# One core: the small gate rows and the low-rank decays of a GLA/mLSTM block as products of stacked split parts, the running maximum in two parts, diagonal scores as column sums

## The chip, the core and the metric

The kernel runs on one core of one Trainium2 chip. A core has a matrix engine (TensorE, PE in the profile; its weight loads are the row PEld), a vector engine (VectorE, DVE), an activation engine (ScalarE, ACT), a general one (GpSimd, POOL), and a queue engine that here mainly issues transfers (SyncE, SP). Each has its own in-order queue, and they meet through semaphores. Work lies in an on-chip memory of 128 partitions; TensorE writes into a second one, PSUM, of which a tile here has at most 512 fp32 columns, and DVE and ACT evict from there. The metric is the device time of one execution in microseconds, the median of several.

## The reference

One layer of a hybrid backbone block over 512 latent tokens with a prefix of 256 context tokens, width 2048. One input projection feeds two groups of four heads each: gated linear attention (GLA) with a decay per channel, and mLSTM with scalar gates. Both scan the tokens in both directions. Their gated outputs go through an output projection and then a SwiGLU MLP with a 3x3 convolution. The change concerns the decays, the gates and one set of scores:

```python
    dec = jnp.einsum('btr,zrk->zbtk', glr, gla_w_lr) + gla_b_lr[:, None, None, :]
    gla_loga = (jax.nn.log_sigmoid(dec.astype(f32)) / GLA_NORMALIZER).reshape(N_DIR, b, t, GLA_HEADS, GLA_DK)
...
        rel = jnp.where(tril[:, :, None], bcum[:, :, :, None, :] - bcum[:, :, None, :, :], -jnp.inf)
        scores = jnp.einsum('bhjk,bhik,bhjik->bhji', qc, kc, jnp.exp(rel))
...
        m_q = jnp.maximum(inter_log, jnp.max(d_log, axis=-1))
        s = jnp.einsum('bhjk,bhik->bhji', qc, kc) * jnp.exp(d_log - m_q[..., None])
```

`glr` has 16 values a token, the low-rank input of the decays; z is the direction. The mLSTM gates are 16 further values a token (input and forget gate, two directions, four heads). On the diagonal of the GLA scores the decay is 1, so a diagonal score is the plain product of a token's query and key.

## The kernel before, in words

Everything lies with channels on the partitions and tokens along the row. A plain fp32 product is written with fp32 operands; the big projections instead cut each fp32 operand into a rounded high part (type F32R) and the F32R remainder, and add three products of such parts. A plain fp32 product of 128 columns shows as two records in the profile, a product of parts as one. All of them stand under the helper's line L98, transposes under L103; so the profile is read here by the names of the tiles. `a` are the accumulators of the projections, `hi_h`, `lo_h`, `hTh`, `hTl`, `hch`, `hcl` their split operands (weights, latent tokens, context tokens).

The first 200 us compute the modulation and the normalised tokens. The stretch from 200 to about 830 us is the recurrent part: GLA heads 0 to 3, then mLSTM heads 4 to 7. `weave` mixes the steps of a head (a generator; each `yield` ends a step and names how much projection work may follow) with the projection products of the next head, and the order of TensorE's instructions is pinned to the order in which the program writes them. The other engines' order is set by a list scheduler, with some evictions raised in priority. While a GLA head runs, `gla_prep` of the next one is advanced by `next(after, None)` at six places of the levels.

The steps that the change touches:

- `small_rows` turns the gathered rows `gm` into `glr`: latent tokens in columns 0 to 511, context tokens behind them. Rows 0 to 15 are the decays' low-rank input, row 16 is ones (for the bias), rows 32 to 47 are the mLSTM gate inputs.
- `gla_prep` loads the head's weights `wlr` (16 rows and the bias row), forms the decays of the latent tokens `dec` (128 channels by 512 tokens, one product a direction) and of the context tokens `cdec` (tokens by channels, two products a direction, one PSUM tile a direction), and puts both through `log_sigmoid`: three passes of ACT (tiles `lt`, `ct`) and one of DVE (`la`, `cla`). `bt` are the running sums of `la`, `csum` the sums of `cla` by products with triangles of ones, `b` and `ends` follow from `bt`.
- `gla` first forms the diagonal scores: `sd` is query times key of a 128-token block, multiplied by twice the identity into `scd`, the first half of the tile `sc`. Then for seven levels `ex` takes the exponentials of differences of `bt`, times query and key, `sl` is their product, and a mask copies part of it into `sc`. At the end `po` multiplies `qi` and `sc` with states and values.
- `ml_gates` picks from `glr` the four rows of a gate and a direction (`pre`, two products a tile in two groups of columns), runs sums and running maxima along the tokens, writes the negated running maximum `negg` (rows 0 to 3 and 32 to 35 for the two directions), transposes rows into columns (`pa`), and spreads the maximum at the end of the context over the partitions (`pgc`, from `dg`).
- `mlstm` spreads the head's row of `negg` over 128 partitions (`pg`, one product a direction) and takes exponentials from it.

Transfers of projection weights (`raw_h`, 512 KB each) and of `wlr` go through SP's queue in its order. Memory of a pool is handed on when the last reader of the tile before is through.

## Time and profile before

| | |
|---|---|
| median of 3 runs | 2513.63 us (2512.5 to 2513.84) |
| the profiled execution | 2511.87 us, its span 2510.1 us |
| granted clock | 0.998 |
| PE busy | 2469.3 us, 98% |
| DVE, ACT, POOL busy | 1815.0, 1024.0, 182.5 us |
| the recurrent part, 200 to 830 us | 630 us, of which PE busy 622.30 us |

The page has numbered parts: the engines' busy time, the span in 40 slices, the queues, the chain of work that ended last, the costliest groups, and the transfers. A row of a timeline gives start, length, engine, line, operation, written tile and read tiles, partitions x elements and type, and how many instructions of a kind follow each other; in brackets stands how long the engine was idle before, and who ended that. Since products overlap, the step between two starts is what a product costs in a stream, not its length. A row of the chain gives start, length and what it was. Buffer numbers are left out.

### The profile page before, as it was taken

The page shows a single profiled execution, that of the slowest core. Times are in us where ns is not written, and L with a number is a line of the kernel's source. Part 1 is how long each engine was busy: PE and PEld are TensorE (multiplying, and loading weights), DVE is VectorE, ACT ScalarE, POOL GpSimd, SP SyncE. Part 2 cuts the span into 40 slices and gives each one's busy share as a digit, 9 for nine tenths or more (in the row PEclk, how much of TensorE's full clock was granted, in tenths as well). Part 3 has the DMA queues.
Part 4 walks back from the last instruction along what each step waited for, and adds up shares of the span by engine and source line. Part 5 has one row for each costly group of instructions (what it writes and reads, how often), then busy time and mean ns, then how long its engine had stood idle before and what let it go on. Part 6 is the DMA issues. An engine that isn't in the chain of part 4 may idle for free.

```text
span 2510.1 us, 39398 instructions
## 1 busy us (share of the span) xinstructions
PE 2469.3 (98%) x15740; PEld 2204.1 (88%) x15740; DVE 1815.0 (72%) x2880; ACT 1024.0 (41%) x1517; POOL 182.5 (7%) x242
## 2 busy tenths in 40 slices
PE   6999999999999999999999999999999999999998
PEld 4887889888987888888989999999999999999997
DVE  6666754554445877858988787878787878787886
ACT  4224543332213233226454444444444444444445
POOL 0000000000000000000020101010101010101022
PEclk9999999999999999999999999999999999999999
DMA  9741011123334878842373737373636363646464
GB/s 385 271 172 42 26 43 51 51 76 125 110 117 155 286 274 304 299 158 99 108 176 101 168 104 166 107 168 104 167 104 166 107 162 108 161 113 160 113 186 135
DMA packets 121552, 372.20 MB, mean 148 GB/s; under 512 B 13908, under 2 KB 18328, under 8 KB 121368
## 3 DMA queue, kind: packets, MB, share of 16 engines
q1 hardware_dynamic: 94680, 318.29, 37.7%
q0 software_dynamic: 25600, 50.34, 11.4%
q8 instruction: 123, 2.02, 0.3%
q10 hardware_dynamic: 1088, 1.05, 0.1%
q14 instruction: 61, 0.50, 0.1%
HBM read 319.30 MB, written 50.33 MB: 147 GB/s over the span
## 4 chain that ended last, share of the span: by engine, by line
PE 85%; issue 9%; DVE 2%; DMA 2%; POOL 1%; ACT 1%; SPq 0%; DVEq 0%; POOLq 0%; ACTq 0%
PE a L98 19%; PE dn L98 17%; PE uv L98 15%; PE ug L98 14%; PE ga L98 7%; PE po L98 4%; PE wo L98 3%; PE sl L98 1%; PE ps_m L98 1%; DMA raw_m<-in_w_mod 1%; PE cst L98 1%; PE s L98 1%; DMA xl<-in_xT 0%; POOL x2d L1269 0%; DMA x2d<-st 0%
## 5 line engine op out<-in xcount | busy, mean ns | idle before, releaser
L98 PE MATMUL dn<-gh,lo_d 128*128 128x512 f32 x672 | 262.3, 390 | 0.3 <-DVE lo_d L93 0.3
L98 PE MATMUL dn<-gh,hi_d 128*128 128x512 f32 x672 | 261.6, 389 | 0.0
L98 PE MATMUL dn<-gl,hi_d 128*128 128x512 f32 x672 | 261.6, 389 | 0.0
L1215 DVE SCALAR_TENSOR_TENSOR cv<-pads,cwt,cv 128x512 f32<-128x512 f32 x344 | 239.5, 748 | 0.6
L1269 POOL DMA_DIRECT2D x2d<-st x160 | 140.1, 928 | 1142.7 <-ACT st L1268 1057.5
L313 DVE SCALAR_TENSOR_TENSOR sum_m<-raw_m,csil,sum_m 128x512 f32<-128x512 f32 x240 | 180.1, 750 | 9.0 <-DMA raw_m<-in_w_mod 3.1
L93 DVE TENSOR_TENSOR lo_buv<-sum_uv,hi_buv 128x1024 fp32r<-128x1024 f32 x80 | 98.0, 1224 | 103.6 <-ACT hi_buv L92 103.6
L98 PEld LDWEIGHTS dn<-gh,lo_d 128*128 128x128 f32 x672 | 126.1, 188 | 28.9 <-DVE lo_d L93 2.6
L98 PE MATMUL a<-hi_h,hTh 128*128 128x256 f32 x512 | 150.4, 294 | 0.5 <-ACT e L406 0.5
L98 PEld LDWEIGHTS dn<-gl,hi_d 128*128 128x128 f32 x672 | 126.2, 188 | 25.9
L98 PEld LDWEIGHTS dn<-gh,hi_d 128*128 128x128 f32 x672 | 126.2, 188 | 25.6
L98 PE MATMUL a<-hi_h,hTl 128*128 128x256 f32 x512 | 144.7, 283 | 0.0
L98 PE MATMUL a<-lo_h,hTh 128*128 128x256 f32 x512 | 144.7, 283 | 0.0
L92 ACT CAST hi_d<-raw_d 128x1024 fp32r<-128x1024 f32 x86 | 88.6, 1030 | 131.9 <-PE ug L98 70.6
L93 DVE TENSOR_TENSOR lo_d<-raw_d,hi_d 128x1024 fp32r<-128x1024 f32 x86 | 102.9, 1196 | 48.1 <-ACT hi_d L92 47.5
L98 PE MATMUL ug<-bth,hi_bug 128*128 128x256 f32 x480 | 136.7, 285 | 0.1
L98 PE MATMUL uv<-bth,lo_buv 128*128 128x256 f32 x480 | 135.9, 283 | 0.8 <-DVE lo_buv L93 0.8
L98 PE MATMUL uv<-bqh,lo_auv 128*128 128x256 f32 x480 | 135.9, 283 | 0.0
L98 PE MATMUL uv<-bth,hi_buv 128*128 128x256 f32 x480 | 135.9, 283 | 0.0
L98 PE MATMUL uv<-bql,hi_auv 128*128 128x256 f32 x480 | 135.8, 283 | 0.0
L98 PE MATMUL ug<-bqh,lo_aug 128*128 128x256 f32 x480 | 135.8, 283 | 0.0
L98 PE MATMUL uv<-btl,hi_buv 128*128 128x256 f32 x480 | 135.8, 283 | 0.0
(379 smaller groups left out, 7347.2 us busy)
## 6 DMA issues: line engine op xcount, KB each, us to landing
raw_m<-in_w_mod SPq DMA_DIRECT2D x192, 512.0 KB, 5.2
raw_d<-in_w_down SPq DMA_DIRECT2D x82, 512.0 KB, 3.4
raw_ug<-in_w_up SPq DMA_DIRECT2D x80, 512.0 KB, 3.5
x2d<-st POOLq DMA_DIRECT2D x160, 256.0 KB, 5.5
raw_uv<-in_w_up SPq DMA_DIRECT2D x80, 512.0 KB, 6.2
raw_h<-in_w_heads SPq DMA_DIRECT2D x64, 512.0 KB, 3.6
raw_ga<-in_w_gates SPq DMA_DIRECT2D x32, 512.0 KB, 4.5
raw_wo<-in_w_out SPq DMA_DIRECT2D x32, 512.0 KB, 4.8
```

The costliest lines, as they stand in the source:

```text
L92: cast[0] = S.copy(hi, x).ins
L93: return V.tensor_tensor(out=lo, in0=x, in1=hi.bitcast(F32), op=ALU.subtract).ins
L98: ins = PE.matmul(*args, **kw)
L313: V.scalar_tensor_tensor(out=parts[0], in0=x, scalar=ck, in1=parts[0], op0=ALU.mult, op1=ALU.add)
L1215: V.scalar_tensor_tensor(out=t3, in0=src, scalar=w, in1=t3, op0=ALU.mult, op1=ALU.add)
L1269: nc.gpsimd.dma_start(x2d[k], t, accum_op=ALU.add)
```

## The change

Every fp32 number can be written as a sum of an F32R high part and an F32R remainder. The change stacks such parts along the contraction, which is short here, so that one product does what several would:

- `glr` becomes a tile of 98 rows of type F32R: high part of the 32 rows, the high part once more, the remainders, and two rows of ones. One product of `gm` with a selection of 96 columns fills PSUM; ACT casts it into all 96 rows, and DVE makes the last 32 the remainder (a column `C_LO` holds −1 there).
- The weights come as 98 rows in HBM; ACT casts, DVE turns rows 32 to 63 and the last into remainders. The raw tile and `wlr` have one buffer each. High by high, high by remainder and remainder by high are then added by one `dec` or `cdec` product.
- The two directions of `cdec` go into one PSUM tile, two products of 256 columns, and one `log_sigmoid`. The step that fell away is an empty `yield`.
- `pre` selects its 36 rows by a matrix `pick`, which is loaded and cast once, and adds high part and remainder by one product.
- `negg` becomes two F32R tiles, `negh` and `negl`, and `pg` two products a direction.
- `sd`: DVE multiplies query and key into `scd`, and four products with one column of ones sum over the channels; the result is spread along the row by the identity, as before.
- `small`, one tile, holds what `csil` and `eps` held; the constants are 128 columns wider.

```diff
@@ -43,8 +43,9 @@
 
 C_ID, C_LS, C_US, C_SEG = (P * i for i in range(4))
 C_SA = C_SEG + T
-C_ONE = C_SA + 32
-C_END = C_ONE + 1
+C_ONE = C_SA + 96
+C_LO = C_ONE + 1
+C_END = C_LO + 64
 
 
 def constants():
@@ -54,8 +55,20 @@
-    c[:, C_SA : C_SA + 32] = i[:, None] % 32 == np.arange(32)[None, :]
+    c[:, C_SA : C_SA + 96] = i[:, None] % 32 == np.arange(96)[None, :] % 32
     c[:, C_ONE] = 1.0
+    c[64:96, C_LO] = -1.0
+    c[32:64, C_LO + 1] = c[97, C_LO + 1] = -1.0
+    return c
+
+
+def picks():
+    c = np.zeros((96, P), np.float32)
+    for t in range(2):
+        for d in range(2):
+            for r in range(4):
+                c[[16 + 8 * d + 4 * t + r, 80 + 8 * d + 4 * t + r], 36 * t + 32 * d + r] = 1.0
+    c[0:36, 72:108] = np.eye(36)
     return c
 
 
@@ -114,9 +127,9 @@
     cst = keep.tile([P, C_END], F32, name="cst")
     cols = keep.tile([P, 148], F32, name="cols")
     msk = keep.tile([P, len(LEVELS), P], U8, name="msk")
-    csil = keep.tile([P, 128], F32, name="csil")[:, 0:KT]
+    small = keep.tile([P, 128], F32, name="small")
+    csil, eps = small[:, 0:KT], small[:, KT : KT + 1]
-    eps = keep.tile([P, 128], F32, name="eps")[:, 0:1]
@@ -477,12 +490,13 @@
     st_h = ExitStack()
     states = pool(st_h, "states")
 
-    glr = states.tile([48, T + TC], F32, name="glr")
+    glr = states.tile([98, T + TC], F32R, name="glr")
 ...
-    negg = states.tile([36, T], F32, name="negg")
+    pick = states.tile([96, 128], F32R, name="pick")
+    negg = [states.tile([36, T], F32R, name=f"neg{p}") for p in "hl"]
@@ -573,7 +587,10 @@
-    V.memset(glr, 1.0)
+    V.tensor_copy(glr[96:98, :], cst[96:98, C_ONE : C_ONE + 1].to_broadcast([2, T + TC]))
+    pickf = mraw.tile([96, 128], F32, name="pickf", tag="raw")
+    nc.sync.dma_start(pickf, a["picks"])
+    V.tensor_copy(pick, pickf)
@@ -591,11 +608,11 @@
 
     def small_rows():
         for c0, n, m in ((0, T, gm[0]), (T, TC, gm[1])):
-            ps = psb(f"glr{c0}", (48, n))
-            mm(ps[0:16, :], cc(C_SA, 16), m, start=True, stop=True)
-            mm(ps[32:48, :], cc(C_SA + 16, 16), m, start=True, stop=True)
-            V.tensor_copy(glr[0:16, c0 : c0 + n], ps[0:16, :])
-            S.copy(glr[32:48, c0 : c0 + n], ps[32:48, :])
+            ps = psb(f"glr{c0}", (96, n))
+            mm(ps, cc(C_SA, 96), m, start=True, stop=True)
+            o = glr[0:96, c0 : c0 + n]
+            S.copy(o, ps)
+            V.scalar_tensor_tensor(out=o, in0=o.bitcast(F32), scalar=cc(C_LO, 1, 96), in1=ps, op0=ALU.mult, op1=ALU.add)
             yield 1.4
 
 
@@ -652,23 +669,27 @@
 
     def gla_prep(h, out):
 
-        wlr = wk2.tile([17, 2, DK], F32, name=f"wlr{h}", tag="wlr")
-        nc.sync.dma_start(wlr, a["w_lr"][h])
+        raw = wtile(f"wlraw{h}", "wlraw", 2, DK)[0:98]
+        nc.sync.dma_start(raw, a["w_lr"][h])
+        wlr = wk.tile([98, 2, DK], F32R, name=f"wlr{h}", tag="wlr")
+        S.copy(wlr, raw)
+        V.scalar_tensor_tensor(out=wlr, in0=wlr.bitcast(F32), scalar=cc(C_LO + 1, 1, 98), in1=raw,
+                               op0=ALU.mult, op1=ALU.add)
         la = wtile(f"la{h}", "la", 2, T)
         t = wtile(f"lt{h}", "tmp", 2, T)
-        cla = wtile(f"cla{h}", "cla", 2, CJ, DK)
-        ct = ytile(15, f"ct{h}", (P, 2, CJ, DK))
+        cla = wtile(f"cla{h}", "cla", CJ, 2, DK)
+        ct = ytile(15, f"ct{h}", (P, CJ, 2, DK))
         for d in range(2):
             ps = psb(f"dec{h}{d}")
-            mm(ps, wlr[:, d, :], glr[0:17, 0:T], start=True, stop=True)
+            mm(ps, wlr[:, d, :], glr[:, 0:T], start=True, stop=True)
             log_sigmoid(la[:, d], ps, t[:, d])
             yield
-        for d in range(2):
-            ps = psb(f"cdec{h}{d}", (P, CJ, DK))
-            for j in range(CJ):
-                mm(ps[:, j, :], glr[0:17, T + P * j : T + P * j + P], wlr[:, d, :], start=True, stop=True)
-            log_sigmoid(cla[:, d], ps, ct[:, d])
-            yield
+        ps = psb(f"cdec{h}", (P, CJ, 2, DK))
+        for j in range(CJ):
+            mm(ps[:, j], glr[:, T + P * j : T + P * j + P], wlr, start=True, stop=True)
+        log_sigmoid(cla, ps, ct)
+        yield
+        yield
 
@@ -682,9 +703,9 @@
             tri = cc(C_LS) if d == 0 else cc(C_US)
             for j in range(CJ):
                 more = j == d
-                mm(ps[:, d, j, :], tri, cla[:, d, j, :], start=True, stop=not more)
+                mm(ps[:, d, j, :], tri, cla[:, j, d, :], start=True, stop=not more)
                 if more:
-                    mm(ps[:, d, j, :], ones, cla[:, d, 1 - j, :], start=False, stop=True)
+                    mm(ps[:, d, j, :], ones, cla[:, 1 - j, d, :], start=False, stop=True)
@@ -740,11 +761,12 @@
         scd, sc1 = sc[:, 0], sc[:, 1]
-        ps = psb(f"sd{h}", (P, TJ, P))
+        mul(scd.rearrange("p a b -> p (a b)"), *qk)
+        ps = psb(f"sd{h}", (P, TJ))
         for j in range(TJ):
-            mm(ps[:, j, :], qk[1][:, P * j : P * j + P], qk[0][:, P * j : P * j + P], start=True, stop=True)
-        V.scalar_tensor_tensor(out=scd, in0=ps, scalar=2.0, in1=ident.unsqueeze(1).to_broadcast([P, TJ, P]),
-                               op0=ALU.mult, op1=ALU.mult)
+            mm(ps[:, j : j + 1], scd[:, j, :], cst[:, C_ONE : C_ONE + 1], start=True, stop=True)
+        V.scalar_tensor_tensor(out=scd, in0=ident.unsqueeze(1).to_broadcast([P, TJ, P]), scalar=2.0,
+                               in1=ps.unsqueeze(2).to_broadcast([P, TJ, P]), op0=ALU.mult, op1=ALU.mult)
@@ -834,9 +856,7 @@
         for t, r in ((0, li), (1, pf)):
             for c0, n, at in ((0, T, lat0), (T, TC, ctx0)):
                 ps = psb(f"pre{t}{c0}", (36, n))
-                for d in range(2):
-                    e = C_ID + 32 + 8 * d + 4 * t
-                    mm(ps[rows[d], :], cst[32:48, e : e + H], glr[32:48, c0 : c0 + n], start=True, stop=True)
+                mm(ps, pick[:, 36 * t : 36 * t + 36], glr[0:96, c0 : c0 + n], start=True, stop=True)
                 for d in range(2):
                     V.tensor_scalar(out=r[rows[d], at[d] : at[d] + n], in0=ps[rows[d], :],
                                     scalar1=bg[rows[d], t : t + 1], scalar2=None, op0=ALU.add)
@@ -869,8 +889,10 @@
             end = TC - 1 if d == 0 else T
-            V.tensor_scalar(out=negg[rows[d], :], in0=gmx[rows[d], lat0[d] : lat0[d] + T], scalar1=-1.0,
-                            scalar2=None, op0=ALU.mult)
+            x = gmx[rows[d], lat0[d] : lat0[d] + T]
+            nh, nl = (n[rows[d], :] for n in negg)
+            V.tensor_scalar(out=nh, in0=x, scalar1=-1.0, scalar2=None, op0=ALU.mult)
+            V.scalar_tensor_tensor(out=nl, in0=x, scalar=-1.0, in1=nh.bitcast(F32), op0=ALU.mult, op1=ALU.subtract)
             V.tensor_scalar(out=dg[rows[d], :], in0=e, scalar1=gmx[rows[d], end : end + 1], scalar2=None, op0=ALU.mult)
             pg = psb(f"pgc{d}", (P, H))
             mm(pg, cst[rows[d], C_ONE : C_ONE + 1].to_broadcast([H, P]), dg[rows[d], :], start=True, stop=True)
@@ -897,8 +919,9 @@
         for d in range(2):
             rows = slice(32 * d, 32 * d + H)
             pg = psb(f"pg{h}{d}")
-            mm(pg, cst[rows, C_ID + 32 * d + hh : C_ID + 32 * d + hh + 1].to_broadcast([H, P]), negg[rows, :],
-                      start=True, stop=True)
+            one = pick[rows, 72 + 32 * d + hh : 73 + 32 * d + hh].to_broadcast([H, P])
+            for n, part in enumerate(negg):
+                mm(pg, one, part[rows, :], start=(n == 0), stop=(n == 1))
             S.activation(qs[:, d, :], pg, AF.Exp, bias=gccol[:, d, hh : hh + 1])
...
-    lr = np.concatenate([gla_w_lr[0], gla_b_lr[0][:, None, :]], 1)
-    r["w_lr"] = lr.reshape(2, 17, H, DK).transpose(2, 1, 0, 3)
+    lr = np.zeros((2, 98, H * DK), np.float32)
+    for row in range(0, 96, 32):
+        lr[:, row : row + 16] = gla_w_lr[0]
+    lr[:, 96:] = gla_b_lr[0][:, None, :]
+    r["w_lr"] = lr.reshape(2, 98, H, DK).transpose(2, 1, 0, 3)
```

The order on TensorE at head 1's preparation, around the second group of `cdec`, before (`sl_6` are the scores of the seventh level, `a_1` and `a_2` projections):

```order
L98 MATMUL a_1_2035<-hTl_950,hi_h_3_2393 128x512
L98 MATMUL a_1_2035<-hTh_949,lo_h_3_2394 128x512
L98 MATMUL cdec_2409<-wlr_2294,glr 128x128 x2
L98 MATMUL sl_6_2422<-ex_6_2416 128x128 x4
L98 MATMUL a_2_2036<-hi_h_3_2393,hTh_939 128x256
L98 MATMUL a_2_2036<-lo_h_3_2394,hTh_939 128x256
```

and after:

```order
L111 MATMUL a_1_2039<-hTl_951,hi_h_3_2395 128x512
L111 MATMUL a_1_2039<-hTh_950,lo_h_3_2396 128x512
L111 MATMUL sl_6_2417<-ex_6_2411 128x128 x4
L111 MATMUL a_2_2040<-hi_h_3_2395,hTh_940 128x256
L111 MATMUL a_2_2040<-lo_h_3_2396,hTh_940 128x256
```

The group has gone, its products having been joined to the first group; `sl_6` follows `a_1` directly.

The order on SP, where the loads of `wlr` for heads 0 and 1 stand, before:

```order
L179 DMA raw_h_0_2045<-in_w_heads 128x1024
L656 DMA wlr_2080<-in_w_lr 17x256
L179 DMA raw_h_1_2149<-in_w_heads 128x1024
L656 DMA wlr_2294<-in_w_lr 17x256
L179 DMA raw_h_2_2264<-in_w_heads 128x1024
L179 DMA raw_h_3_2391<-in_w_heads 128x1024
L179 DMA raw_h_4_2507<-in_w_heads 128x1024
L179 DMA raw_h_5_2678<-in_w_heads 128x1024
L656 DMA wlr_2745<-in_w_lr 17x256
L179 DMA raw_h_6_2801<-in_w_heads 128x1024
```

and after:

```order
L192 DMA raw_h_0_2048<-in_w_heads 128x1024
L192 DMA raw_h_1_2147<-in_w_heads 128x1024
L192 DMA raw_h_2_2263<-in_w_heads 128x1024
L192 DMA raw_h_3_2393<-in_w_heads 128x1024
L192 DMA raw_h_4_2502<-in_w_heads 128x1024
L192 DMA raw_h_5_2674<-in_w_heads 128x1024
L673 DMA wlraw_2082<-in_w_lr 98x256
L673 DMA wlraw_2293<-in_w_lr 98x256
L192 DMA raw_h_6_2800<-in_w_heads 128x1024
L673 DMA wlraw_2741<-in_w_lr 98x256
```

The loads of heads 0 and 1 have moved from behind the first and second `raw_h` of the piece to behind the sixth, where `raw_h_6` follows them; the load of head 2 now stands behind `raw_h_6` instead of ahead of it.

The order on DVE around head 1's diagonal scores, before (`ob` takes the output of head 0 from `po`, `sc` from `sd` is the diagonal, `qi` belongs to head 1):

```order
L818 COPY ob_2536<-po_0_2537 128x256
L818 COPY ob_2536<-po_1_2546 128x256
L818 COPY ob_2536<-po_2_2561 128x256
L84 TENSOR_TENSOR qi_2704<-qi_2704,e_0_1256 128x1024
L818 COPY ob_2536<-po_3_2570 128x256
L746 SCALAR_TENSOR_TENSOR sc_2589<-sd_2593,cst 128x512
```

and after:

```order
L840 COPY ob_2531<-po_0_2532 128x256
L840 COPY ob_2531<-po_1_2541 128x256
L840 COPY ob_2531<-po_2_2556 128x256
L97 TENSOR_TENSOR sc_2584<-e_0_1257,e_1_1266 128x512
L97 TENSOR_TENSOR qi_2700<-qi_2700,e_0_1257 128x1024
L840 COPY ob_2531<-po_3_2565 128x256
L768 SCALAR_TENSOR_TENSOR sc_2584<-cst,sd_2589 128x512
```

The product of query and key into `sc` stands behind the third `ob` and ahead of `qi`; the evictions from `po` and `sd` follow in the order that they had.

More of the change, by code (lines that the diff above doesn't have):

```diff
@@ L1393, in arrange @@
     r["masks"] = masks()
+    r["picks"] = picks()
     r["cols"] = np.concatenate([col(g_norm1[0]), col(g_norm2[0]), col(b_mod[0]), col(g_final), col(gla_g_norm[0]),
```

## The prediction

> **What bounds the kernel now.** I read the page's head and busy lines first, then a table of windows over the stretch in which the edited lines run, then the waits of TensorE there.
>
> ```profile
> span 2510.1 us, 39398 instructions
> PE 2469.3 (98%) x15740; PEld 2204.1 (88%) x15740; DVE 1815.0 (72%) x2880; ACT 1024.0 (41%) x1517; POOL 182.5 (7%) x242
> ```
>
> ```profile
> 200.00:222.00 22.00, 18.57 (x105) 13.75 (x100) 13.42 (x28) 11.94 (x23) 0.00 (x0) 1.00 0.08 26
> 222.00:262.00 40.00, 39.08 (x247) 34.33 (x247) 35.79 (x57) 22.75 (x46) 0.00 (x0) 1.00 0.08 28
> 262.00:330.00 68.00, 66.78 (x395) 59.20 (x394) 46.17 (x89) 34.01 (x77) 0.00 (x0) 1.00 0.10 32
> 330.00:405.00 75.00, 75.00 (x461) 67.62 (x460) 40.46 (x63) 31.91 (x62) 0.73 (x1) 1.00 0.14 43
> 520.00:830.00 310.00, 309.52 (x1704) 267.63 (x1704) 156.47 (x332) 87.88 (x168) 15.38 (x33) 1.00 0.38 124
> ```
>
> ```profile
> PE sl L98 <- DVE ex L84: 3.2, 3, 1.7
> PE cdec L98 <- DVE la L635: 1.7, 2, 1.1
> ```
>
> The columns of the windows are length, then PE, PEld, DVE, ACT and POOL busy, granted clock (1.00 in all), DMA share and GB/s. PE has no free time from 330 to 405 and half a microsecond from 520 to 830, so a microsecond taken off PE there is one off the end. From 200 to 222 it is idle for 3.4 us, and in 222:262 DVE is busy for 35.8 of 40: there the vector chain decides, and the waits name it (columns: total, times, longest). The sum is made against the profiled execution, 2511.87 us (1.76 us around the span), and is carried to the median of 2513.63 us by the same 1.76 us.
>
> **Unit prices.** From the timeline of PE (start, length; the step between starts is the price, since lengths overlap):
>
> ```profile
> 481.18 0.28 PE L98 MATMUL a<-hi_h,hTl 128*128 128x256 f32 x1
> 481.30 0.28 PE L98 MATMUL a<-hi_h,hTh 128*128 128x256 f32 x1
> ...
> 487.86 0.39 PE L98 MATMUL a<-hTl,hi_h 128*128 128x512 f32 x1
> 488.08 0.39 PE L98 MATMUL a<-hTh,lo_h 128*128 128x512 f32 x1
> 488.40 1.02 PE L98 MATMUL pre<-glr,cst 16*4 16x512 f32 x4
> 489.35 0.50 PE L98 MATMUL a<-hTh,hi_h 128*128 128x512 f32 x1
> ...
> 490.94 0.60 PE L98 MATMUL pre<-glr,cst 16*4 16x256 f32 x4
> 491.47 0.39 PE L98 MATMUL a<-hi_h,hTh 128*128 128x256 f32 x1
> ```
>
> The `a` products are split parts, as the new `dec`, `cdec`, `pre` and `pg` are: one record costs 0.12 us at 256 columns and 0.22 to 0.23 us at 512. The chain has the plain ones:
>
> ```profile
> 234.18 1.05 PE dec L98 x2
> ...
> 298.12 0.65 PE cdec L98 x4
> ```
>
> **dec and cdec.** A `dec` falls from 1.05 to 0.23 us: −0.82 each, two a head. A head's `cdec` falls from two groups of 0.65 to two records of 0.12: −1.06. That is −2.7 us of PE a head, four heads. What of it arrives:
>
> - 330:405 prepares head 3, with PE never idle: −2.7, whole.
> - 262:330 prepares head 2; its last third waits for vector work after `cdec`. The two `dec` count whole (−1.6), of `cdec` I take two thirds (−0.7): −2.3, bounds −1.0 and −2.7.
> - Head 0 and the preparation of head 1, 200:262. The chain of head 0 and its tail:
>
> ```profile
> 206.15 1.06 PE dec L98 x2
> ...
> 209.53 0.70 DVE la L635
> ...
> 221.82 1.13 PE sl L98 x8
> ```
>
> ```profile
> 251.58 0.43 DVE cla L635
> 252.05 1.60 PE csum L98 x12
> ```
>
> From 206.15 on the chain leaves PE and goes through ACT and DVE until 221.82, so head 0's 2.7 us mostly become wait. Only the start of the first decay moves up, since both `dec` no longer stand before the ACT work; I take −0.4. Then head 1's preparation frees 2.7 us of PE, but DVE (89% busy) gains one `cla` of 0.43 us that becomes part of a longer one, loses 0.43 us to the new weight part (same size, so the same row), and still has to bring `ex` to the next `sl`. What comes free is that `csum` no longer waits for the second `cla` at 252.05. I take −1.6, so −2.0 for the window, with bounds 0 (the vector chain keeps its time) and −3.9 (2.7 of PE, the 0.9 us that PE idles in 222:262, and 0.3 more at head 0).
>
> **pre.** The rows give 0.95 and 0.53 us, two each: 2.96. After: 0.23 + 0.12, twice, 0.70. Each group has an empty 0.09 us ahead of it (488.08 + 0.23 to 488.40), and about as much behind: up to 0.7 more. So −2.3 to −3.0; I take −2.7. Behind it stands a chain that does not get shorter:
>
> ```profile
> 505.48 0.41 DVE L872 TENSOR_SCALAR negg<-pf 4x512 f32<-4x512 f32 x1
> 506.69 0.21 DVE L874 TENSOR_SCALAR dg<-cst,pf 4x4 f32<-4x4 f32 x1
> ```
>
> ```profile
> 507.11 0.53 PE L103 MATMUL pa<-cst,li 4*128 4x4 f32 x6
> 507.75 0.36 PE L98 MATMUL pgc<-dg,cst 4*128 4x4 f32 x2
> ```
>
> `pgc` needs `dg`, done at 506.90: 0.85 us of slack. PE comes 2.7 earlier. DVE comes between 0 and 2.7 earlier (it evicts the same four tiles); I take 2.0. The low half of the maximum adds one DVE operation of 0.41 ahead of `dg`. Slack 0.85 − 0.41 − 0.7 = −0.3: a new wait of 0.3 us. So −2.4, bounds −1.5 and −3.0.
>
> **pg.** Timeline of PE at the first of the four heads:
>
> ```profile
> 519.72 0.28 PE L98 MATMUL a<-hi_h,hTl 128*128 128x256 f32 x1
> 519.93 1.13 PE L98 MATMUL pg<-negg,cst 4*128 4x512 f32 x4
> 520.99 0.44 PE L98 MATMUL a<-hi_h,hch 128*128 128x384 f32 x1
> ```
>
> Both directions, four records, take 1.06 us, as long as the single `dec` with two: they run side by side, in two groups of rows. Four split records take 0.92 us in file and 0.47 in two pairs side by side. The nearest row is `pg` itself, on the same rows, so I take side by side, with a little for gaps: −0.55 a head, −2.2 for four; bounds −0.6 and −2.4. The second negation itself is the 0.41 us counted above.
>
> **sd.** Four products of 128 columns become one DVE product (`q` times `k`) and four products of one column:
>
> ```profile
> 271.05 1.89 PE L98 MATMUL po<-v,sc 128*128 128x256 f32 x8
> 272.78 1.05 PE L98 MATMUL sd<-e,e 128*128 128x128 f32 x8
> 273.59 0.36 PE L98 MATMUL a<-hi_h,hTh 128*128 128x256 f32 x1
> ```
>
> ```profile
> 1140.64 3.10 PE L98 MATMUL ps_rms<-cst,sqsq 128*128 128x1 f32 x24 [0.21 <-DVE sqsq L87]
> ```
>
> A record of `sd` costs 0.81 / 8 = 0.10 us; one with a single column costs 3.10 / 24 = 0.13 us in the row of `ps_rms`. So eight of them save nothing; bounds 0 and +0.2 a head. The Trainium skill, TensorEngine Tiling (Array Packing), section Performance Considerations, says that a product of one column takes as long as one of 60, about 60 cycles; at the 2.4 GHz of its page TensorE: Matmul & The Clock Gate eight records would by that take some 0.2 us (an estimate), and the sum would fall by 2.4 us more. The row of `ps_rms` disagrees.
>
> The new DVE product writes into the tile that the previous head's `po` reads. In heads 0, 2 and 3 it stands many operations ahead of `sd`. In head 1 `sd` follows `po` directly. The reads of that tile end about a quarter into the group at 271.05, some 271.6; an evict of the same 128x512 size (`la`, 0.70) brings 272.3 plus hand-overs. `sd` wants PE at 272.78: no wait, bound +1.0 if the release comes with the group's end. Four extra products of 0.7 lie in DVE's idle time.
>
> **glr, weights, constants.** `glr` goes from two products side by side to one wider one, and the evictions are two passes over 96 rows instead of one copy each; PE has `a` behind it: 0. The constants load grows by 65.5 KB, at the start, when PE waits for loads. The weights' load grows to 100 KB and moves down SP's queue, behind the fourth `raw_h`:
>
> ```profile
> raw_h<-in_w_heads SPq DMA_DIRECT2D x64, 512.0 KB, 3.6
> ```
>
> ```profile
> 170.91 24.02 SPq L179 DMA_DIRECT2D raw_h<-in_w_heads  x4
> ...
> 218.25 28.26 SPq L179 DMA_DIRECT2D raw_h<-in_w_heads  x3
> ```
>
> By the landing row 65.5 KB cost at most 0.5 us; I take +0.2. The fourth `raw_h` is issued at 194.9, so head 0's weights land by about 199 to 203, then a cast and a DVE pass (0.4 each), and `dec` wants them at 206.15: hidden with 2 us or more. Later heads ask for theirs tens of microseconds ahead.
>
> **Sum.** −2.0 − 2.3 − 2.7 − 2.4 − 2.2 + 0 + 0.2 = −11.4 us: the profiled execution at 2500.5, the median at 2502.2 us.
>
> **Rivals.**
> - *All of it arrives.* Eight `dec` 6.6, four `cdec` 4.2, `pre` 3.0, `pg` 2.4, and about 1 us of the waits on DVE: −17.2 + 0.2, 2496.6 us. For it: PE at 98%. Against: the chain through ACT and DVE from 206 to 222.
> - *The vector chains keep their time, and `pg` runs in file.* 200:262 nothing, 262:330 −1.0, 330:405 −2.7, `pre` −1.5, `pg` −0.6, `sd` +1.0 at head 1, preparation +0.5, start +0.5: −3.8, 2509.8 us. For it: DVE at 89% in 222:262.
> - *One column is next to free*: `sd` gives back its whole 0.81 us in four heads, −3.2 on top of the sum: 2499.0 us. Against: 0.13 us a record in `ps_rms`. It is the rule of the Trainium skill's tiling page, above, taken to its end.
> - *Slower: head 0's weights come late.* SP's queue stands before the `raw_h` of 218.25 for a buffer. If the weights' load is held until then (it also waits for memory that PE must have left), it lands at 218.6 + 3.6, is ready 0.8 later at 223.0, and `dec` starts 16.9 us late, all of it PE standing: −11.4 + 16.9, 2519.1 us. It decides from 16.4 us of lateness on (`dec` at 222.6). Against: in SP's order it stands ahead of that `raw_h`, not behind.
>
> **How the numbers follow.** Changes under 0.2% (5.0 us) can't be told from none. Chances: the forecast 0.50 (own range 2499 to 2505.5), all of it 0.17, one column cheap 0.04, vector chains 0.19, late weights 0.10. The first three are faster (0.71), and a quarter of the vector case, whose terms spread over 2506 to 2512, is too (0.05): 0.76 faster, 0.14 within, 0.10 slower. The range takes in the first case whole, nearly all of "all of it" and most of the vector case, and leaves out late weights and the tails: 2495.5 to 2511.
>
> **What would show it.** In the profile after: `dec` at 0.23 us a record, `cdec` at 0.12, and the head 3 stage shorter by 2.7; `pre` 0.2 and 0.1; four `pg` records within 0.5 us (in file: 0.9); `sd` still near 0.8; head 0's `sl` only some 0.4 earlier, with a wait on ACT or DVE ahead of it; a short wait at `pgc`. Wrong would be: a wait of PE at head 0's `dec` for the weights, one at head 1's `sd` for the DVE product, or `sd` at a quarter of its time.

## The result and the profile after

The changed kernel takes 2503.59 us (median of five runs, 2501.22 to 2507.01) against 2513.63 us: ratio 0.9964, 95% interval 0.9953 to 0.9975. That is 10.0 us less, where 11.4 were forecast (2502.2 us, range 2495.5 to 2511). In a second comparison both were slower, with the same ratio: 2506.02 against 2514.87 us, 0.9964 (0.9953 to 0.9976).

The profiled execution is one of the slow ones of its kernel: 2507.01 us, span 2505.3. The span is therefore only 4.8 us shorter than before, so the two profiles are compared stage by stage. First the page's head and the windows that answer to those of before (length, then PE, PEld, DVE, ACT and POOL busy, granted clock, DMA share, GB/s):

```profile
span 2505.3 us, 39311 instructions
PE 2458.9 (98%) x15692; PEld 2205.6 (88%) x15692; DVE 1819.1 (73%) x2887; ACT 1021.3 (41%) x1509; POOL 182.2 (7%) x242
```

```profile
200.00:222.00 22.00, 17.67 (x102) 14.48 (x95) 14.02 (x28) 11.93 (x22) 0.00 (x0) 0.92 0.11 34
222.00:262.00 40.00, 37.54 (x246) 34.65 (x246) 37.46 (x60) 22.79 (x44) 0.00 (x0) 1.00 0.10 32
330.00:405.00 75.00, 75.00 (x477) 69.91 (x476) 40.34 (x67) 29.76 (x59) 0.74 (x1) 1.00 0.16 50
```

The clock in the first row is 0.92, where it was 1.00. In 222:262 DVE has come to 37.5 us of 40 and PE's free time has grown from 0.9 to 2.5 us: the chain there is a vector chain now. From 330 to 405 PE still has no free time.

Since TensorE's order is the same, the same instruction can be looked up in two timelines. Starts on PE, in us; the last two columns are the shift against before in the changed kernel (its first profile, and its second, of the run `after_again` below):

| first start of | before | after | shift | shift, second profile |
|---|---|---|---|---|
| `glr` | 199.94 | 200.54 | +0.60 | +0.92 |
| `dec`, head 0 | 206.08 | 206.11 | +0.03 | +0.34 |
| `po`, head 0 | 261.03 | 259.54 | −1.49 | −1.65 |
| `yt`, head 1 | 330.73 | 327.62 | −3.11 | −3.29 |
| `yt`, head 2 | 410.97 | 404.40 | −6.57 | −6.75 |
| `pre` | 484.08 | 477.50 | −6.58 | −6.76 |
| `pa` | 507.11 | 497.60 | −9.51 | −9.69 |
| `pg`, head 4 | 519.93 | 514.79 | −5.14 | −5.48 |
| last `yt` | 814.39 | 807.59 | −6.80 | −7.13 |
| `ug` (after the second norm) | 1148.74 | 1143.28 | −5.46 | −5.86 |

The gain grows as forecast up to `pa`, then 4.4 us of it are lost between `pa` and `pg` (4.2 in the second profile), and another 1.3 us at the second norm. The products themselves are as cheap as forecast. From the timeline of PE (start, length, idle before in brackets):

```profile
359.25 0.40 PE L111 MATMUL a<-hTh,lo_h 128*128 128x512 f32 x1
359.49 0.39 PE L111 MATMUL dec<-glr,wlr 98*128 98x512 f32 x1
359.72 1.05 PE L111 MATMUL sl<-ex 128*128 128x128 f32 x8
...
364.74 0.28 PE L111 MATMUL a<-hi_h,hTl 128*128 128x256 f32 x1
364.86 0.40 PE L111 MATMUL cdec<-wlr,glr 98*128 98x256 f32 x2
365.10 1.06 PE L111 MATMUL sl<-ex 128*128 128x128 f32 x8
...
480.31 0.40 PE L111 MATMUL pre<-glr,pick 96*36 96x512 f32 x1
480.54 0.40 PE L111 MATMUL a<-hTh,hi_h 128*128 128x512 f32 x1
...
481.94 0.28 PE L111 MATMUL pre<-glr,pick 96*36 96x256 f32 x1
482.06 0.29 PE L111 MATMUL a<-hi_h,hTh 128*128 128x256 f32 x1
```

`dec` costs 0.23 us, both records of `cdec` 0.24, `pre` 0.23 and 0.12. The gaps ahead of these products (0.09 us before) are gone too. Behind `pa` the profile shows what went wrong:

```profile
497.60 0.53 PE L116 MATMUL pa<-cst,li 4*128 4x4 f32 x6
498.55 0.41 PE L116 MATMUL pa<-cst,cum 4*128 4x4 f32 x4 [0.42 <-DVE cum L100]
499.38 0.35 PE L111 MATMUL pgc<-dg,cst 4*128 4x4 f32 x2 [0.43 <-DVE dg L896]
...
500.83 0.28 PE L111 MATMUL a<-hi_h,hTh 128*128 128x256 f32 x1
500.95 0.35 PE L111 MATMUL a<-lo_h,hTh 128*128 128x256 f32 x1
501.09 0.42 PE L111 MATMUL a<-hi_h,hTl 128*128 128x256 f32 x1
501.92 0.80 PE L116 MATMUL pa<-cst,li 4*128 4x4 f32 x6 [0.41 <-DVE gccol L899]
...
504.31 0.41 PE L111 MATMUL a<-hi_h,hTh 128*128 128x256 f32 x1
504.52 0.41 PE L111 MATMUL a<-lo_h,hTh 128*128 128x256 f32 x1
```

There are three waits of 0.4 us, and from 501 on an `a` record of 256 columns costs 0.21 us instead of 0.12. Only the first two waits lie ahead of 501; the third falls into the slower stretch. The windows of the same profile give the granted clock of that stretch:

```profile
496.00:501.00 5.00, 4.15 (x31) 3.42 (x30) 4.91 (x9) 1.46 (x4) 0.00 (x0) 1.00 0.00 0
501.00:508.00 7.00, 6.59 (x33) 6.28 (x33) 2.07 (x8) 1.07 (x4) 0.00 (x0) 0.51 0.26 77
508.00:512.00 4.00, 4.00 (x22) 3.49 (x21) 2.42 (x6) 1.50 (x3) 0.00 (x0) 1.00 0.00 0
```

For 6.8 us the granted clock is half. That is the larger part of the 4.4 us: 1.3 of waits, some 3.1 of clock. While TensorE has work, the clock fell below 0.97 in three places of this profile: 211 to 214 us (head 0, behind a wait of 1.8 us for `la` ahead of `cdec`), 501 to 508, and 1136 to 1143 us (behind `ps_rms`). Before, it fell in one, at 1143 to 1147 us. DVE's timeline shows what PE waits for:

```profile
497.21 0.41 DVE L894 TENSOR_SCALAR negh<-pf 4x512 fp32r<-4x512 f32 x1
497.56 0.94 DVE L100 TENSOR_TENSOR cum<-cum,pf 36x768 f32<-36x768 f32 x1
498.42 0.67 DVE L895 SCALAR_TENSOR_TENSOR negl<-pf,negh 4x512 fp32r<-4x512 f32 x1
499.02 0.21 DVE L896 TENSOR_SCALAR dg<-cst,pf 4x4 f32<-4x4 f32 x1
```

The new `negl` stands ahead of `dg`, for which `pgc` waits, but behind `cum`, for which the first wait is. DVE's first negation starts 8.27 us earlier than before (505.48), PE's `pa` 9.51: DVE has come up less than PE.

### The profile page after: what moved, and what is told of

The parts are those of the page before. It is cut to its first block, busy times and chain, and to the rows that moved or that the text cites. A ratio compares the mean times of both kernels' runs of the same rounds, so it can differ in the third digit from the quotient of the medians.

```text
span 2505.3 us, 39311 instructions
## 1 busy us (share of the span) xinstructions
PE 2458.9 (98%) x15692; PEld 2205.6 (88%) x15692; DVE 1819.1 (73%) x2887; ACT 1021.3 (41%) x1509; POOL 182.2 (7%) x242
## 3 DMA queue, kind: packets, MB, share of 16 engines
q0 software_dynamic: 25600, 50.34, 11.4%
q10 hardware_dynamic: 1088, 1.05, 0.1%
## 4 chain that ended last, share of the span: by engine, by line
PE 84%; issue 9%; DVE 3%; DMA 2%; ACT 1%; POOL 0%; SPq 0%; DVEq 0%; POOLq 0%; ACTq 0%
PE a L111 18%; PE uv L111 16%; PE dn L111 15%; PE ug L111 15%; PE ga L111 7%; PE po L111 4%; PE wo L111 3%; PE sl L111 1%; PE ps_m L111 1%; DVE cv L1238 1%; DMA raw_m<-in_w_mod 1%; DMA raw_uv<-in_w_up 1%; PE cst L111 1%; PE s L111 1%; DVE lo_d L106 0%
## 5 line engine op out<-in xcount | busy, mean ns | idle before, releaser
L326 DVE SCALAR_TENSOR_TENSOR sum_m<-raw_m,small,sum_m 128x512 f32<-128x512 f32 x240 | 180.1, 750 | 10.3 <-DMA raw_m<-in_w_mod 4.8
```

The costliest lines, as they stand in the source:

```text
L326: V.scalar_tensor_tensor(out=parts[0], in0=x, scalar=ck, in1=parts[0], op0=ALU.mult, op1=ALU.add)
```

## The experiments

Two theories stood after the first profile. The clock theory: PE's new waits at `pa` and `pgc`, which come from DVE, pull the clock down, and taking them away brings 4 us. The chance theory: half clocks come at random places and only the 1.3 us of waits belong to the change.

**The changed kernel again.**

> The changed kernel once more, to see whether its stretches of half granted clock come at the same places. If PE's new waits cause them (theory 1), the granted clock is again 0.50 for 3 to 7 us right behind the waits at the start of head 0 (about 210 us) and at pa and pgc (about 501 us), and pg starts near 514.8. If they come by chance (theory 2), they lie elsewhere or are absent, and pg starts near 511.5.

Measured: 2506.02 us (2501.94 to 2507.97, six runs). Its profile has the half clock at the same place (from 500.4 to 507.3 us), none at head 0, and the one at the second norm; `pg` starts at 514.45. Ahead of the half clock stand the first two waits, at `cum` and `dg`; the third is absent:

```profile
496.00:501.00 5.00, 4.15 (x29) 3.47 (x28) 4.91 (x9) 1.46 (x4) 0.00 (x0) 0.94 0.00 0
501.00:508.00 7.00, 6.92 (x36) 6.61 (x35) 1.90 (x8) 1.21 (x5) 0.00 (x0) 0.55 0.24 77
```

So the place behind `pa` repeats, the one at head 0 doesn't, though its wait of 1.8 us ahead of `cdec` is the same. Two profiles of kernels below that keep the two waits (`u_sd`, `u_cdec`) have 6.8 us of half clock there as well.

**The parts of the maximum formed late (`m1`).**

```diff
-            V.tensor_scalar(out=nh, in0=x, scalar1=-1.0, scalar2=None, op0=ALU.mult)
-            V.scalar_tensor_tensor(out=nl, in0=x, scalar=-1.0, in1=nh.bitcast(F32), op0=ALU.mult, op1=ALU.subtract)
...
-            V.tensor_copy(gccol[:, d, :], pg)
+            spread = V.tensor_copy(gccol[:, d, :], pg).ins
             yield 1.4
+        for d in range(2):
+            x = gmx[rows[d], lat0[d] : lat0[d] + T]
+            nh, nl = (n[rows[d], :] for n in negg)
+            with tc.issue_after(spread):
+                V.tensor_scalar(out=nh, in0=x, scalar1=-1.0, scalar2=None, op0=ALU.mult)
+                V.scalar_tensor_tensor(out=nl, in0=x, scalar=-1.0, in1=nh.bitcast(F32), op0=ALU.mult,
+                                       op1=ALU.subtract)
```

> The changed kernel with both parts of the negated running maximum formed behind the last gccol, so that dg and cum come earlier on DVE and PE's order stays. Theory 1: PE's waits at pa and pgc fall from 1.3 us to about 0.3, the half clock at 501 us goes, pg starts 4 us earlier, near 510.8; the time falls by up to 4 us against the changed kernel, to about 2500 us. Theory 2: only the waits go, pg near 513.8, the half clock still comes in some executions.

Measured: 2502.59 us (2501.09 to 2503.69), 3.4 us under the changed kernel of the same batch. PE's waits are down to 0.2 us, and the clock stays whole. Timeline of PE, and windows, of `m1`:

```profile
497.15 0.53 PE L116 MATMUL pa<-cst,li 4*128 4x4 f32 x6
497.90 0.41 PE L116 MATMUL pa<-cst,cum 4*128 4x4 f32 x4 [0.21 <-DVE cum L100]
498.17 0.36 PE L111 MATMUL pgc<-dg,cst 4*128 4x4 f32 x2
500.08 0.53 PE L116 MATMUL pa<-cst,li 4*128 4x4 f32 x6
```

```profile
496.00:501.00 5.00, 4.79 (x42) 4.06 (x40) 4.35 (x9) 1.45 (x6) 0.00 (x0) 1.00 0.11 23
501.00:508.00 7.00, 7.00 (x43) 6.48 (x43) 5.26 (x14) 2.35 (x7) 0.00 (x0) 1.00 0.17 61
```

From `pa` to `pg` the shift goes from −9.96 to −9.57 us: 0.4 lost where the changed kernel loses 4.4. This is what the clock theory expects, to 0.4 us (`pg` at 510.36, expected 510.8). One profile could be chance, but all thirteen of this document agree: the four with waits of 0.4 us at both `cum` and `dg` have the half clock behind them, and of the eight others without a wait made by hand (five with one wait of 0.2 us, `u_pg` with one of 0.4, the kernel before and `b_wide` with none) not one has it there. The loss of the changed kernel behind `pa` is thus of its own making: between `pre` and `pa` PE gains 2.9 us and DVE only 1.7, and the negations, to which a second part of 0.67 us a direction has been added, stand ahead of what PE waits for.

**One wait made in the kernel before (`b_wait`).**

```diff
-            V.tensor_tensor_scan(out=o, data0=x, data1=x, initial=0.0, op0=ALU.max, op1=ALU.bypass)
+            for _ in range(1 + d):
+                V.tensor_tensor_scan(out=o, data0=x, data1=x, initial=0.0, op0=ALU.max, op1=ALU.bypass)
```

> The kernel before, with the second scan of the running maximum run twice (same result), so that cum comes 1.9 us later and PE waits about 1.2 us in the middle of pa, where it did not wait. Theory 1: the granted clock halves behind the wait for 3 to 7 us, and the time rises by 1.2 plus 2 to 3.5 us, to about 2517 us. Theory 2: the wait costs 1.2 us and no more, 2514.8 us, clock 1.00 there.

Measured: 2516.67 us, ratio to before 1.0006 (0.9996 to 1.0015), ten runs from 2512.71 to 2522.09. The profile is that of the execution of 2522.09 us. Timeline of PE, then windows:

```profile
508.23 0.53 PE L103 MATMUL pa<-cst,li 4*128 4x4 f32 x6
509.97 0.40 PE L103 MATMUL pa<-cst,cum 4*128 4x4 f32 x4 [1.20 <-DVE cum L87]
```

```profile
504.00:511.00 7.00, 5.80 (x37) 4.91 (x37) 6.81 (x9) 2.51 (x5) 0.00 (x0) 1.00 0.14 55
511.00:518.00 7.00, 7.00 (x39) 6.76 (x38) 2.24 (x8) 1.07 (x4) 0.00 (x0) 0.54 0.25 75
```

A wait of 1.2 us set there by hand is followed by the same 6.8 us of half clock, and from `pa` to `pg` the kernel loses 4.3 us (shift +1.12 to +5.45): as much as the changed kernel. But some of its runs lie at the time of before with a mean clock of 0.998, so the wait seems to make the half clock likely, not certain (these executions have no trace); the median is only 1.8 us up, and the interval of its ratio includes 1. Two further half clocks of this profile, at 215 and 1300 us, lie far from the wait. Both theories had a part: the wait sets the place, and chance, it seems, decides in which execution.

**A chunk of projections ahead of head 0's `cdec` (`m3`).**

```diff
-        for need in (0, 1.4, 0, 3, 1, 0):
+        for need in (0, 3, 0, 1.4, 1, 0):
```

(on top of `m1`.)

> m1, and one chunk of projection products (six of 384 columns, 1.0 us) moved ahead of head 0's cdec, where PE stood 1.8 us. Theory 1: the wait falls to about 0.8 us, the half clock of 211 to 214 us goes, and the first sl comes up to 1 us earlier; the time about 2499 us. Theory 2: the half clock is as likely as before; the first sl does not move.

Measured: 2502.46 us (2501.08 to 2505.2), the time of `m1`. The wait ahead of `cdec` fell to 0.75 us as expected, but the rest failed: the first `sl` came at 222.81, 1.4 us later than in `m1`, and a half clock came all the same, at 215 to 219 us. Timelines of PE and of ACT show why:

```profile
210.03 0.50 PE L111 MATMUL cdec<-wlr,glr 98*128 98x256 f32 x2 [0.75 <-DVE la L652]
215.65 2.93 PE L111 MATMUL csum<-cla,cst 128*128 128x128 f32 x12 [4.06 <-DVE cla L652]
```

```profile
211.88 1.03 ACT L105 CAST hi_h<-raw_h 128x1024 fp32r<-128x1024 f32 x1
212.82 0.63 ACT L651 ACTIVATE ct<-ct 128x512 f32<-128x512 f32 x1
```

A cast of projection weights (`hi_h`) now runs ahead of the last pass of `ct`, and on DVE `lo_h` ahead of `cla`, which starts at 214.91 where `m1` has 213.37. PE has no projections left to fill the time, stands for 4.06 us, and `csum` then falls into the half clock (2.93 us, 1.60 in `m1`). Head 0's start is a chain through ACT and DVE, and PE's work only lies in its gaps.

**The diagonal scores as before (`u_sd`).**

```diff
-        mul(scd.rearrange("p a b -> p (a b)"), *qk)
-        ps = psb(f"sd{h}", (P, TJ))
+        ps = psb(f"sd{h}", (P, TJ, P))
         for j in range(TJ):
-            mm(ps[:, j : j + 1], scd[:, j, :], cst[:, C_ONE : C_ONE + 1], start=True, stop=True)
+            mm(ps[:, j, :], qk[1][:, P * j : P * j + P], qk[0][:, P * j : P * j + P], start=True, stop=True)
...
```

> The changed kernel with the diagonal scores as before (four products of 128 columns, no product on DVE). By the prediction the step is worth nothing: sd takes 0.81 us as it does with one column, head 1's po-to-sd step is no shorter, the shift of the stages against the kernel before stays within 0.2 us at every head, and the time is that of the changed kernel. Rival, one column is cheap: 2.4 to 3.2 us more than the changed kernel.

Measured: 2503.60 us (2500.97 to 2506.45). At head 1, the changed kernel and `u_sd`, each from its timeline of PE:

```profile
271.37 1.05 PE L111 MATMUL sd<-cst,sc 128*128 128x1 f32 x8
272.29 0.36 PE L111 MATMUL a<-hi_h,hTh 128*128 128x256 f32 x1
```

```profile
271.24 1.05 PE L111 MATMUL sd<-e,e 128*128 128x128 f32 x8
272.05 0.36 PE L111 MATMUL a<-hi_h,hTh 128*128 128x256 f32 x1
```

One column takes 0.92 us here, 128 columns 0.81; in the other three heads both take 0.81 to 0.82. The step is worth nothing, or a loss of 0.1 us. The DVE product ran at 270.62 to 271.31, ahead of `sd`, as forecast. One column is not cheap here. The weight loads (PEld) of the changed kernel show a possible reason:

```profile
271.37 0.97 PEld L111 LDWEIGHTS sd<-cst,sc 128*128 128x128 f32 x8 [0.32 <-DVE sc L97]
```

Each of the eight records has a weight load of its own of 128 columns, and the loads follow each other as slowly as the records; no run separates the load from the product.

**The maximum in one fp32 part (`u_pg`).**

```diff
-    negg = [states.tile([36, T], F32R, name=f"neg{p}") for p in "hl"]
+    negg = states.tile([36, T], F32, name="negg")
...
-            for n, part in enumerate(negg):
-                mm(pg, one, part[rows, :], start=(n == 0), stop=(n == 1))
+            mm(pg, cst[rows, C_ID + 32 * d + hh : C_ID + 32 * d + hh + 1].to_broadcast([H, P]), negg[rows, :],
+                      start=True, stop=True)
```

> The changed kernel with the running maximum in one fp32 part. pg costs 0.42 us more in each of four heads, +1.7 us. DVE does 1.3 us less ahead of dg and gccol, so PE's waits at pa and pgc fall from 1.3 to about 0.5 us. Clock theory: the half clock at 501 us then comes in fewer executions or not at all, so that undoing this part costs nothing or even gains up to 2 us. Chance theory: 1 us slower than the changed kernel.

Measured: 2502.47 us (2501.56 to 2503.00). Each `pg` costs 0.4 us more again, but PE waits only once at `pa` (0.42 us), no half clock follows, and `pg` of head 4 starts at 510.76. The last `yt` stands at −9.16 us, against −6.80 and −7.13 in the changed kernel and −11.22 in `m1`. So the wait at `cum` doesn't come from the second part; the one at `dg` does, and one wait of 0.4 us was not enough for a half clock in this profile. As the change makes it, the running maximum in two parts costs more in the waits that it causes than its cheaper products bring; placed late, it brings 2 us by the shift at the last `yt`. The medians of `u_pg` and `m1`, of different batches, do not show that (both 0.9951 of before).

**The four `pg` records in another order (`m5`).**

```diff
-            for n, part in enumerate(negg):
-                mm(pg, one, part[rows, :], start=(n == 0), stop=(n == 1))
+        pgs = [psb(f"pg{h}{d}") for d in range(2)]
+        for n, part in enumerate(negg):
+            for d in range(2):
...
+                mm(pgs[d], one, part[rows, :], start=(n == 0), stop=(n == 1))
```

(on top of `m1`.)

> m1, and the four pg records ordered high, high, low, low with the two directions (two groups of rows) in turn, where they were high, low, high, low. If records in different groups of rows run side by side only when they follow each other, the four take 0.47 us instead of 0.67, and each mLSTM head gains 0.2 us, 0.8 in all. If not, pg stays at 0.67.

Measured: 2500.52 us (2498.84 to 2501.10). `pg` took 0.67 us as before. But the profile of the changed kernel already has the order that `m5` sets, though the program writes high, low, high, low there:

```profile
514.79 0.50 PE L111 MATMUL pg<-negh,pick 4*128 4x512 f32 x2
515.13 0.40 PE L111 MATMUL pg<-negl,pick 4*128 4x512 f32 x2
515.46 0.44 PE L111 MATMUL a<-hi_h,hch 128*128 128x384 f32 x1
```

In `after`, `m1` and `m5` alike the two high records start within 0.01 us of each other, then the two low ones. They do run side by side; a pair takes 0.33 us, where a single record of 512 columns takes 0.23. Why it takes more stays open, and `m5` tested no other order. The shift at the last `yt` is that of `m1`, −11.25 and −11.22. The profiles differ by 4.2 us behind it: 2.5 at the second norm, where the clock did not fall in `m5`, and 1.6 in the MLP, not followed further. This is the size of what chance can do between two kernels whose recurrent parts are alike.

**`cdec` in two groups again (`u_cdec`).**

```diff
-        ps = psb(f"cdec{h}", (P, CJ, 2, DK))
-        for j in range(CJ):
-            mm(ps[:, j], glr[:, T + P * j : T + P * j + P], wlr, start=True, stop=True)
-        log_sigmoid(cla, ps, ct)
-        yield
-        yield
+        for d in range(2):
+            ps = psb(f"cdec{h}{d}", (P, CJ, DK))
+            for j in range(CJ):
+                mm(ps[:, j, :], glr[:, T + P * j : T + P * j + P], wlr[:, d, :], start=True, stop=True)
+            log_sigmoid(cla[:, :, d, :], ps, ct[:, :, d, :])
+            yield
```

> The changed kernel with cdec in two groups a head again (split parts, 128 columns, one log_sigmoid a direction), the rest as changed. If cdec's gain comes from the cheaper records alone, the stage of head 2 (330 to 405 us before) is shorter by the same 3.2 us as in the changed kernel; if joining the groups carries a part of it (a group's switch, a wait for a second PSUM tile), it is 2.4 to 2.8 us, and the first sl of head 0 comes up to 0.5 us later. Time within 1 to 2 us above the changed kernel, apart from the half clock at 501 us, which stays.

Measured: 2504.65 us (2502.35 to 2510.37). From the `sl` ahead of head 2 to the one at its end (312 to 383 us before) the shift grows by 3.30 us (−1.08 to −4.38), in the changed kernel by 3.21 (−3.38 to −6.59). Counted from the next `sl` on (340 us before) it is 3.30 against 3.47. So the cheaper records alone bring nearly all of the gain, and joining the groups adds 0.2 us at most there. The first `sl` of head 0 moved 0.65 us ahead of its `dec`'s shift, where the joined form without a half clock gives 0.54: the expected delay did not come. The half clock behind `pa` stayed, as expected. Further ones at 222 and at 297 us fell into this profile, so the total says little.

**Wide sums (`m4`, `b_wide`).** The half clock behind `ps_rms` stood in the profiles of before and of the changed kernel, though PE is busy there. Its 24 records have one column each.

```diff
-        ps = psb(f"ps_{name}", (P, nj))
+        wide = psb(f"ps_{name}", (P, nj, P))
+        ps = wide[:, :, 0]
...
-                mm(ps[:, j : j + 1], sq[:, P * j : P * j + P], cst[:, C_ONE : C_ONE + 1],
+                mm(wide[:, j, :], sq[:, P * j : P * j + P], ones,
```

> m1, and the sums over channels of the second norm (ps_rms) and of the last one with 128 columns of ones in place of one, the same number of records, every column the same sum. If the clock goes by columns streamed and not by the engine being busy, the 6.6 us of half clock behind ps_rms (1131 to 1138 us in m1) go, 2 to 3.5 us off m1, about 2499.5 us. If it goes by busy time, they stay, and the time is that of m1, 2502.6 us.

> The kernel before with the sums of the two norms as in m4 (128 columns of ones for one). If one-column records pull the clock down, the 4 to 5 us of half clock at 1142 us go and the time falls by 1.5 to 2.5 us against the kernel before. If the absence in m4 was chance, it stays, and the time is the same within 0.5 us.

Measured: `m4` 2499.18 us (2498.33 to 2500.08), ratio to before 0.9939 (0.9924 to 0.9954). `b_wide` 2512.82 us, ratio 0.9995 (0.9986 to 1.0003). First the changed kernel, then `m4`, then the kernel before, then `b_wide`, windows behind `ps_rms`:

```profile
1135.00:1142.00 7.00, 6.99 (x36) 6.90 (x36) 2.76 (x8) 1.21 (x5) 0.36 (x1) 0.56 0.49 161
```

```profile
1131.00:1138.00 7.00, 6.68 (x55) 6.20 (x55) 4.60 (x10) 3.10 (x7) 0.63 (x2) 1.00 0.55 187
```

```profile
1142.00:1148.00 6.00, 5.99 (x40) 5.90 (x40) 2.58 (x8) 1.02 (x4) 0.17 (x1) 0.72 0.53 178
```

```profile
1141.00:1148.00 7.00, 6.56 (x54) 6.25 (x54) 4.60 (x11) 3.10 (x7) 0.86 (x2) 1.00 0.58 198
```

`ps_rms` takes as long as before (3.10 us with one column, 3.08 in `b_wide`), and the clock does not fall behind it. From `ps_rms` to the first `ug` it is 7.02 us in both wide kernels, 8.10 in the kernel before and 9.45 in the changed one, whose half clock there lasted 6.8 us instead of 3.4. With one column ten profiles at that point are at hand: seven have a half clock there; `u_sd`, `m5` and `u_cdec` don't, and take 6.9 us for the step, so that width itself gains nothing. With 128 columns there are three (`m6` below too), and none has it. That speaks for the columns, but none of three beside seven of ten doesn't make it certain, and the time of `b_wide` is 1.4 us lower with an interval that includes no change.

**The best of the parts (`m6`)**: `m4` with the diagonal scores of `u_sd`.

> m4 with the diagonal scores as before (no product on DVE), as the best of the parts: dec, cdec, pre and pg as changed, the maximum's parts formed late, wide sums. By the reading that the sd step is worth nothing, it has the time of m4, 2499.2 us, within 1 us, some 0.6% under the kernel before.

Measured: 2500.46 us (2499.19 to 2501.36), ratio 0.9943 (0.9931 to 0.9955): 1.3 us above `m4`, where at most 1 us was expected. `m4` remains the fastest measured, 0.6% under the kernel before, and 4 to 7 us under the two medians of the changed one.

## Why the prediction was right, and where a step failed

- **dec and cdec.** Prices as forecast: 0.23 us and 0.24 us, from 1.05 and 1.30. Head 3's preparation gained 3.46 us (−3.11 to −6.57) instead of 2.7: the gaps around these groups went too. Head 2's gained 1.62 (−1.49 to −3.11) instead of 2.3, since PE now waits there for 1.8 us, 1.27 of it at one `sl` for `la`, where it had waited for 0.8. Together 5.1 against 5.0: the two errors cancel, which is luck.
- **200:262.** Forecast −2.0. Where no half clock came it was −2.0 (`after_again` −1.99, `m1` −2.01, from `dec` to `po`); in the first profile, with one, −1.5. Head 0's first `sl` gained 0.54 without it, 0.4 had been taken. The wait of head 1's `csum` for `cla` went, as forecast; PE's free time in 222:262 grew by 1.5 us, with new waits of 0.79 and 1.37 us at `sl` for `ex`: there the vector chain took back part of what the products had freed.
- **glr and the start.** Forecast 0 and +0.2. From `glr` to `dec` the changed kernels are 0.57 us faster, a gain that was missed: the two wide products, each with the record behind it, take 0.35 us less in all than the pairs, and the gaps of 0.09 us ahead of the second `glr` and of `dec` are gone. The start came 0.60 to 0.92 us late in both profiles, but `b_wait`, whose beginning is the old one, came 0.64 late as well, and `m6` 0.18 early: the loads at the start vary more than the term.
- **pre.** From `pre` to `pa` PE gained 2.93 us (bounds 2.3 to 3.0). The step that failed stands behind them: a new wait of 0.3 us was forecast at `pgc`. It was three waits of 0.4 us, at `cum`, `dg` and `gccol` (two in the second profile). DVE came 1.7 us earlier, not 2.0 as taken; the second part took 0.67 us, not the 0.41 of the first that it was priced by; and no slack was worked out for `cum`, which the first wait is for and which stands behind a negation as well.
- **The clock**, which appears nowhere in the sum: 3.1 us behind `pa`, 0.5 at head 0, 1.3 more than before at the second norm in the first profile. The kernel before has a granted clock of 1.00 in every window that the prediction shows, and the prediction took the price of a wait to be its length.
- **pg.** −0.41 us a head (the shift goes −5.14, −5.55; the last `yt` −6.80), −1.7 against −2.2. The four records took 0.67 us, between the two sums of the prediction (0.47 and 0.92). They ran side by side as forecast, but a pair took 0.33 us, and it had been priced at the 0.23 of a single record.
- **sd.** Forecast 0, measured 0 to +0.1. The rule of the Trainium skill, TensorEngine Tiling (Array Packing), Performance Considerations, that a product of one column takes as long as one of 60, some 60 cycles, gave a price that these records do not reach: 0.81 us for eight, 0.92 at head 1. Each has a weight load of its own, so the trace does not show whether the product or its load sets that.
- **Late weights.** Did not come: the cast ran at 202.97 and the DVE part ended at 203.89, 2.2 us ahead of `dec`.

The sum without clock, by these shifts, is −0.6 (glr) − 2.0 − 1.6 − 3.5 − 2.9 + 1.3 − 1.7 = −11.0 us plus the start's scatter, next to −11.4. That it comes so close is in part luck: two errors of opposite sign at heads 2 and 3, a missed gain at `glr`, and a wait four times as long. What the median lacks to it is about what half clocks take, and how many come differs between executions: the eleven of the changed kernel go from 2501.2 us (mean clock 0.997) to 2508.0 (0.994). Only two of them have a trace, with three and two half clocks; for the others the mean clock is all there is.

## What to carry to other kernels

A DVE operation put ahead of something that TensorE waits for costs its length once the slack is used up, and waits of TensorE of a microsecond in all can cost three more through the clock, as they did here; so look up in the order what stands behind a new operation, and form late what is needed late. Where products get cheaper on the engine that bounds, ask of each engine that feeds it whether its slack is larger than the gain. When a kernel's executions scatter, lay its instruction starts beside those of the other kernel and read the granted clock between two that drift apart.

## What the runs showed of the hardware

Two waits of 0.4 us within 1.3 us, among records of 4 columns, were followed by 6.8 us at a granted clock of 0.50, in four profiles of four; one wait of 1.2 us by 6.8 us; one of 0.4 us (`u_pg`) by none. In the 3.4 us ahead of the half clock PE was busy for 2.55 us in the changed kernel and for 2.20 in `b_wait`. 24 records of one column, with PE busy nearly all the time, were followed by 3.4 or 6.8 us in seven profiles of ten. In none of these cases did PE stand for longer than 1.2 us at a time. The Trainium skill, TensorE: Matmul & The Clock Gate, Part 1, tells of a free-running window of some 3.4 us, after an idle one of which the clock is halved. The lengths agree: from 200 us on and while PE has work, every half clock in the thirteen profiles lasts 3.4 us or 6.8, one such window or two, and a window that runs freely would explain that the same wait sometimes has no such effect. That the window must be idle doesn't agree: here a partly idle one was enough, and narrow records seem to count as idle, which no run here settles. How little is enough stays open. So does whether head 0's half clock belongs to the change: it came in nine profiles of thirteen, `b_wait` and `b_wide` among them, which are the kernel before up to there.
